# A smaller VectorE share of search work and a larger one of routing work per U tile; head-norm rows and positions in one transfer each

## The chip, the cores and the metric

One NeuronCore of a Trainium2 chip runs the kernel. TensorE (PE in the rows, PEld for its weight loads), VectorE (DVE), ScalarE (ACT), GpSimd (POOL) and SyncE (SP) each work through their own instructions in order, and wait for each other at semaphores; transfers are issued by SP alone and go through 16 DMA engines. The metric is the device time of one execution in microseconds (us); the lower the better. "Before" is the kernel without the change.

## The reference

One decoder layer on 256 tokens of width 1024: an input projection, two groups of attention heads, an output projection, and then a product-key expert layer (PEER). The change touches the gains of the head norms, the positions, and the search in PEER.

```python
proj = rmsnorm(x, norm1_gain) @ w_in            # split into two head groups
q = apply_rope(rmsnorm(q, q_gain), cos, sin)    # group A: 8 heads of 64; keys the same way
...
h = x + mixed
# PEER, 8 heads, 128 + 128 sub-keys each, 16384 experts
q = _rms((xt @ w_q).reshape(T, 8, 256))
s1, s2 = q_half1 . sub_keys1, q_half2 . sub_keys2
v1, i1 = top_k(s1, 16); v2, i2 = top_k(s2, 16)
vals, ci = top_k(v1[:, None] + v2[None, :], 16)
e = i1[ci // 16] * 128 + i2[ci % 16]; g = softmax(vals)
a = xt . expert_u[e]; y = (g * gelu(a)) @ expert_v[e]
```

## The kernel before

**No gather.** The expert part doesn't gather rows: it computes the scores of all 16384 experts for all 256 tokens (128 **U tiles** of 128 experts), multiplies them by a routing matrix that is zero except at the chosen experts, and multiplies the product with all of `peer_v` (128 V tiles). Products are made of float32 numbers split in two parts, `hi` (ACT, L769) and `lo` = value - hi (L772), so a U tile is 24 matmuls of 256 columns in three passes of eight: hi with hi, hi with lo, and last lo with hi (`xproj`, L1101). The `lo` of a tile is needed at its third pass, 16 matmuls after its start.

**The pipeline.** Step s of the loop issues the load of tile s+5, splits tile s+3 (`split`: hi on ACT, lo on POOL while `state["single"]` is true, else on DVE) and multiplies tile s; there are three buffers for loaded tiles and four for hi and for lo. 16 tiles of `peer_w_q` (queries) come first, then 128 U tiles (j = 0 to 127), then 128 V tiles (L1474).

**Work beside the tiles.** Between tiles, DVE does the rest of PEER, as a generator (`work_steps`) of pieces with a cost each, written down in the code: for each half of the tokens the search (`topk_steps`): 16 rounds over the sub-keys and 8 over the candidates (0.95 + 0.6 us each in the code's figures), both with `single` true; then, with `single` false, a few steps on indices (to L1253: "ranks"; L1256 to L1264: "cells"), the look-up of the indices (L1268 to L1277) and the softmax's end. Then three transposes on PE (`rT`), casts on DVE (L1297 to L1299), and the second half the same way. After both, 64 **routing groups** of 4 tokens: one-hot vectors on DVE (`oh`, L1305 and L1309), 8 matmuls on PE (`g`, L1317), and the product of the result with the columns of scores that are there already (`route_out`, L1330 on DVE; ACT copies it into columns that are still empty, L1332). From then on a pair of U tiles also has its scores multiplied by the routing columns on POOL (L1449). `work_for(share)` after each tile adds a share to a credit and takes pieces from the generator until the credit is used up:

```python
td = state["routed"]
work_for(2.95 - (1.3 if on_vector.get(s + 3) else 0))
```

So the share is 2.95 us a tile, less 1.3 if the tile's `lo` is on DVE. Where everything stands on each engine is set by this table of costs when the program is built. At U tile 4 a short block is put between (`sums`): the norms of the queries, with a power on POOL (`rq`, L151) between two DVE steps (L1378 to L1380 and L1383).

**The front of the kernel.** SP issues transfers in a written order. Three transfers (`load_gA`, L807 to L809) spread the gains of the head norms, one row of 64 numbers each, over 128 partitions and 8 + 2 + 2 heads (`gA`). They stand between the load of `wu` (L877) and that of the third weight group `win` (L258 called by `load_win(3)`), after which come `w2` and `load_win(4)`. `gB` (L856, 256 numbers of the same tensor to 128 partitions) is loaded earlier. DVE scales `gA` (L910) before it works on the gates and norms of the first projection (L381, L369, L372 to L377); ACT makes their sums (L366 to L368) and then the hi part of `win` (L279), and POOL its lo part (L274).

Of the kernel before, what the change touches and what calls it, by code (L numbers as in the profile page):

```python
# [48 lines left out]
P_N = 43  # L49


R_Q = 0
R_KS = 64
R_KW = 128
R_KC = 192
R_BQ = 256
R_BK = 352
R_N = 448

WIN_GROUPS = (256, 184, 256, 256, 256, 256, 256)  # L60

# [25 lines left out]
def body(tc, nc, ap, dbg=None):  # L87
    V, A, T, G, S = nc.vector, nc.scalar, nc.tensor, nc.gpsimd, nc.sync
# [6 lines left out]
    with ExitStack() as ctx:  # L95
# [33 lines left out]
        def accum(name):  # L129
            return acc.tile([128, 512], F32, tag="acc", name=name)  # L130
# [34 lines left out]
        x = xx[:, 0:2048].rearrange("p (t d) -> p t d", t=2)  # L165
# [4 lines left out]
        con = cst.tile([128, C_N], F32, name="con")  # L170
        ident = con[:, C_ID:C_ID + 128]
        one = con[:, C_ONE:C_ONE + 1]
        pp = cst.tile([128, P_N], F32, name="pp")
        posi = cst.tile([128, 3], I32, name="posi")
# [6 lines left out]
        w2 = wsm[:, 2560:2816].rearrange("p (a b n) -> p a b n", a=2, b=2)  # L181
        gA = wsm[:, 2816:3584].rearrange("p (h d) -> p h d", h=12)
# [557 lines left out]
        raws, parts, pend, on_vector = {}, {}, {}, {}  # L740
# [37 lines left out]
        h = x  # L778
        hs = nc.dram_tensor("hs", (256, 1024), F32, kind="Internal").ap()

        with tc.manual_schedule():

            def load_x(tt):
                for q in range(2):
                    S.dma_start(out=x[:, tt, q * 512:(q + 1) * 512], in_=ap["x"][tt * 128:(tt + 1) * 128, q * 512:(q + 1) * 512])

            win = {}

            def load_win(gi):
                win[gi] = load_pack(ap["win"][:, offs[gi]:offs[gi + 1]], WIN_GROUPS[gi], "win", 2 if gi else 4)  # L790

            def open_win(gi):
                win[gi] = split_pack(win[gi], 2 + gi % 2, WIN_GROUPS[gi], "win%d" % gi)

            def split_win(gi, q, e, what="hl"):
                win[gi][1](q, e, what)

            def load_pos():
                for tt in range(2):
                    S.dma_start(out=posi[:, tt:tt + 1], in_=bass.AP(tensor=ap["pos"].tensor, offset=tt * 128, ap=[[1, 128], [1, 1]]))  # L800
                for g in range(2):
                    S.dma_start(out=posi[g * 32:g * 32 + 15, 2:3], in_=bass.AP(tensor=ap["pos"].tensor, offset=31, ap=[[16, 15], [1, 1]]))

            rows = ap["rows"].tensor

            def load_gA():
                S.dma_start(out=gA[:, 0:8, :], in_=bass.AP(tensor=rows, offset=R_Q, ap=[[0, 128], [0, 8], [1, 64]]))  # L807
                S.dma_start(out=gA[:, 8:10, :], in_=bass.AP(tensor=rows, offset=R_KS, ap=[[0, 128], [0, 2], [1, 64]]))
                S.dma_start(out=gA[:, 10:12, :], in_=bass.AP(tensor=rows, offset=R_KW, ap=[[0, 128], [0, 2], [1, 64]]))  # L809

            def sumsq(tt, e):
                if e is A:
                    A.activation(out=r_sq2(), in_=x[:, tt, :], func=AF.Square, accum_out=ss1[:, tt:tt + 1])
                else:
                    V.scalar_tensor_tensor(r_sq2(), x[:, tt, :], 1.0, x[:, tt, :], op0=ALU.mult, op1=ALU.mult, accum_out=ss1[:, tt:tt + 1])

            def norm1():
                rsqrt(rs1, ss1, 1024.0, 128, 2)
                V.tensor_scalar(nrs1, rs1, -1.0, None, op0=ALU.mult)
                V.tensor_copy(rsrep, rs1[:, :, None].broadcast_to((128, 2, 128)))  # L820

            def masks():
                V.tensor_copy(trim, con[:, C_TRI:C_TRI + 128])
                V.tensor_copy(idb, ident)

            def w0(q, e, what):
                win[0][1].part(q, e, what)

            G.memset(posi, 0)
            G.memset(cm[:, 2048:3328], 0.0)  # L830
            A.activation(out=misc[:, 118:119], in_=mhalf[:, 0:1], func=AF.Square)
            tx = [transposed_split(x[:, tt, :], P_G1, xnT, tt, (lambda k, n, a=(fe, scrB)[tt]: a[:, k * 128:(k + n) * 128].rearrange("p (k t) -> p k t", k=n)), lo=V) for tt in range(2)]
            lows = [accum("low"), accum("low")]
            ss1 = small([128, 2], "n_ss")
            low0 = lambda tt: do(mm_pack(lows[tt][:, 0:256], tt, win[0][0]))
            load_x(0)
            S.dma_start(out=ident, in_=ap["con"][:, C_ID:C_ID + 128])
            S.dma_start(out=pp, in_=ap["pp"])
            load_x(1)
            load_win(0)  # L840
            open_win(0)
            next(tx[0])
            next(tx[0])
            next(tx[0])
            next(tx[0])
            w0(0, G, "h")
            w0(1, G, "h")
            load_win(1)
            open_win(1)
            next(tx[1])  # L850
            next(tx[1])
            w0(1, G, "l")
            do(tx[0])
            next(tx[1])
            w0(2, G, "h")
            S.dma_start(out=gB, in_=bass.AP(tensor=rows, offset=R_KC, ap=[[0, 128], [1, 256]]))  # L856
            next(tx[1])
            sumsq(1, V)
            w0(2, V, "l")
            load_pos()  # L860
            load_win(2)
            w0(3, G, "h")
            split_win(1, 0, None, "h")
            split_win(1, 1, None, "h")
            w0(3, V, "l")
            w0(0, G, "l")
            G.memset(Z, 0.0)
            G.memset(zer, 0.0)
            S.dma_start(out=con[:, 128:C_N], in_=ap["con"][:, 128:C_N])
            split_win(1, 1, G, "l")  # L870
            do(tx[1])
            sumsq(0, A)
            split_win(1, 0, V, "l")
            low0(0)
            V.tensor_scalar(gB[:, 64:160], gB[:, 64:160], float(np.float32(96 ** -0.5)), None, op0=ALU.mult)
            norm1()
            S.dma_start(out=wsm[:, 0:2560], in_=ap["wu"])  # L877
            masks()
            rope_tables()
# [472 lines left out]
        def work_for(share):  # L1352
            credit[0] = min(credit[0] + share, 4.0)
            while credit[0] > 0:
                c = next(work, None)
                if c is None:
                    break
                credit[0] -= c
# [61 lines left out]
        for s in range(NQ, NQ + NU):  # L1420
            j = s - NQ
            load(s + 5)
            split(s + 3)
            if s % 2 == 0:
                b = bank("a")
            xproj(b[:, (s % 2) * 256:(s % 2) * 256 + 256], s, xtT)
            if j == 126:
                for _ in work:
                    pass
                wsplit(0)  # L1430
                wsplit(1)
            if j == 0:
                pend["scores"]()
                qsum = sums()
            if j in (2, 4):
                next(qsum)
            if s % 2:
                td = state["routed"]
                dst = col(j - 1, 2)
                bv = b.rearrange("p (j t) -> p j t", j=2)  # L1440
                if td < 256:
                    A.activation(out=dst[:, :, td:], in_=bv[:, :, td:], func=AF.Gelu_apprx_tanh)  # L1442
                if td > 0:
                    if j < 127:
                        a = ring.tile([128, 2, 256], F32, tag="w", name="gl", bufs=2)
                    else:
                        a = raw("gl")[:, 0:512].rearrange("p (j t) -> p j t", j=2)
                    A.activation(out=a[:, :, :td], in_=bv[:, :, :td], func=AF.Gelu_apprx_tanh)  # L1448
                    (G if j < 127 else V).tensor_tensor(dst[:, :, :td], a[:, :, :td], dst[:, :, :td], op=ALU.mult)  # L1449
                state["done"] = j + 1  # L1450
            td = state["routed"]
            work_for(2.95 - (1.3 if on_vector.get(s + 3) else 0))


        ya = [[bank("y") for n in range(2)] for tt in range(2)]
# [36 lines left out]
def layout(x, positions, norm1_gain, w_in,  # L1492
# [5 lines left out]
    n = np.asarray  # L1498
# [8 lines left out]
    win = np.concatenate([w[:, :, g].transpose(1, 0, 2).reshape(128, -1) for g in groups], axis=1)  # L1507
# [2 lines left out]
    pp = np.concatenate([col(norm1_gain, 8), col(norm2_gain, 8), oga, col(out_gain_b, 4),  # L1510
                         col(mla_q_lora_gain, 2), col(mla_kv_lora_gain, 1),
                         n(cmp_pos)[0].reshape(16, 128).T], axis=1)
    rows = np.concatenate([n(v)[0] for v in (nsa_q_gain, nsa_ks_gain, nsa_kw_gain, nsa_kc_gain, mla_q_gain, mla_k_gain)])[None, :]
    wukv = n(mla_w_ukv)[0].reshape(128, 8, 2, 64).transpose(0, 2, 1, 3).reshape(128, 1024)
    wu = np.concatenate([n(mla_w_uq)[0].reshape(2, 128, 768).transpose(1, 0, 2).reshape(128, 1536), wukv], axis=1)
    w1 = np.stack([n(m)[0].reshape(16, 128, 256).transpose(1, 0, 2).reshape(128, 4096) for m in (cmp_k_w1, cmp_v_w1)])
# [6 lines left out]
    keys = n(peer_sub_keys)[0].reshape(16, 128, 128).transpose(2, 0, 1).reshape(128, 2048)  # L1523
    u = n(peer_u)[0].reshape(128, 128, 8, 128).transpose(1, 3, 2, 0).reshape(128, 128, 1024)
    v = n(peer_v)[0].reshape(128, 131072)
    d = dict(x=n(x)[0], pos=n(positions), con=_constants(), pp=pp, rows=rows, win=win, wu=wu, w1=w1, w2=w2,
             wout=wout, wq=wq, keys=keys, u=u, v=v)
    return {k: np.ascontiguousarray(a) for k, a in d.items()}

# [20 lines left out]
```

## Time and profile before

| | |
|---|---|
| time, median of 3 runs | 981.76 us (980.24 to 984.21) |
| the profiled execution | 981.5 us, of which the span of the profile is 979.7 us |
| PE busy | 944.3 us (96%) |
| DVE busy | 723.3 us (74%) |
| ACT, POOL busy | 500.4 us (51%), 185.4 us (19%) |
| DMA, mean rate over the span | 170 GB/s |

The span runs from the first to the last instruction of the profiled execution; some 1.8 us of its time lie outside. Busy shares are means over stages that differ: the front and attention (to 176 us), queries (to 219.5), U tiles (to 627.5) and V tiles.

### The profile page before, as it was taken

Reading aid. Unit: us, or ns where it says so; the run is one execution under the profiler, and the core shown is the slowest. Engines: PE = TensorE matmul, PEld = TensorE weight load, DVE = VectorE, ACT = ScalarE, POOL = GpSimd, SP = SyncE. Lnnn points to the kernel's source line nnn. Section 1 sums busy time; section 2 is a strip of 40 time slices with the busy share of each in tenths; the row PEclk is TensorE's granted clock in tenths of the full one; section 3 lists DMA queues with packets and bytes.
Section 4 is the critical chain, followed back from the end, with each engine's and each line's share of the span. In section 5 each row is a group of like instructions: output and inputs, shape, how many; then the busy total and the mean of one; then the engine's idle time right before and its main releaser. Section 6 shows DMA issues by size and latency. Waiting matters only on the chain.

```text
span 979.7 us, 17225 instructions
## 1 busy us (share of the span) xinstructions
PE 944.3 (96%) x6657; PEld 853.9 (87%) x6657; DVE 723.3 (74%) x1403; ACT 500.4 (51%) x924; POOL 185.4 (19%) x151
## 2 busy tenths in 40 slices
PE   7699899999899899999999999999999999999998
PEld 6587678999899899999999999988888888888886
DVE  6577988777989987888889997566666666666664
ACT  4445766656355445454544444455555555555552
POOL 5462524267049000000111111100000000000000
PEclk9899999999899899999999999999999999999999
DMA  7623421654466375455555555566665666566554
GB/s 239 211 89 103 175 66 52 207 169 134 151 207 198 115 214 170 154 157 166 159 169 166 155 155 181 180 193 194 193 194 193 194 194 193 194 193 194 193 195 149
DMA packets 48958, 166.74 MB, mean 170 GB/s; under 512 B 7276, under 2 KB 8300, under 8 KB 48620
## 3 DMA queue, kind: packets, MB, share of 16 engines
q1 hardware_dynamic: 48876, 165.64, 53.5%
q8 instruction: 52, 0.85, 0.3%
q14 instruction: 30, 0.25, 0.1%
HBM read 163.52 MB, written 2.10 MB: 169 GB/s over the span
## 4 chain that ended last, share of the span: by engine, by line
PE 77%; DVE 11%; DMA 5%; POOL 3%; ACT 1%; issue 1%; SPq 1%; DVEq 0%; POOLq 0%; ACTq 0%
PE y L1474 36%; PE a L1101 28%; PE q L1101 4%; PE g L1317 3%; DMA win<-win 3%; PE wo L980 1%; DVE lo L772 1%; DMA raw<-u 1%; PE s L1410 1%; PE ak L316 1%; POOL b_rs L151 1%; DMA B<-keys 1%; DVE B L1217 1%; DVE B L1218 1%; PE oA L697 1%
## 5 line engine op out<-in xcount | busy, mean ns | idle before, releaser
L772 DVE TENSOR_TENSOR lo<-raw,hi 128x1024 fp32r<-128x1024 f32 x238 | 291.2, 1227 | 96.2 <-ACT hi L769 94.3
L769 ACT ACTIVATE hi<-raw 128x1024 fp32r<-128x1024 f32 x266 | 280.0, 1054 | 56.8 <-DMA raw<-u 52.5
L1474 PE MATMUL y<-hi,w 128*128 128x512 f32 x1024 | 274.6, 389 | 0.0
L1101 PE MATMUL a<-xtT,hi 128*128 128x256 f32 x2048 | 268.2, 284 | 0.0
L1101 PEld LDWEIGHTS a<-xtT,hi 128*128 128x128 f32 x2048 | 250.6, 191 | 0.4 <-issue 0.4
L1474 PEld LDWEIGHTS y<-hi,w 128*128 128x128 f32 x1024 | 192.0, 188 | 40.1 <-ACT w L1204 0.2
L1474 PE MATMUL y<-lo,w 128*128 128x512 f32 x512 | 158.4, 389 | 0.0
L1101 PE MATMUL a<-xtT,lo 128*128 128x256 f32 x1024 | 142.4, 282 | 8.1 <-DVE lo L772 8.1
L1204 ACT ACTIVATE w<-B 128x256 fp32r<-128x256 f32 x128 | 53.5, 418 | 171.2 <-PE y L1474 171.1
L1101 PEld LDWEIGHTS a<-xtT,lo 128*128 128x128 f32 x1024 | 130.6, 192 | 8.5 <-DVE lo L772 8.5
L1474 PEld LDWEIGHTS y<-lo,w 128*128 128x128 f32 x512 | 96.1, 188 | 20.0
L1205 DVE TENSOR_TENSOR w<-B,w 128x256 fp32r<-128x256 f32 x128 | 54.4, 426 | 70.1 <-ACT w L1204 70.1
L1449 POOL TENSOR_TENSOR B<-gl,B 128x512 f32<-128x512 f32 (+37 forms) x40 | 32.0, 801 | 273.7 <-ACT gl L1448 273.7
L772 POOL TENSOR_TENSOR lo<-raw,hi 128x1024 fp32r<-128x1024 f32 x28 | 67.3, 2410 | 47.1 <-ACT hi L769 46.7
L1332 ACT ACTIVATE B<-g 128x64 f32<-128x64 f32 (+32 forms) x120 | 24.2, 250 | 72.6 <-DVE B L1330 72.6
L1442 ACT ACTIVATE B<-a 128x512 f32<-128x512 f32 (+37 forms) x60 | 27.7, 461 | 62.6 <-PE a L1101 62.6
L1305 DVE TENSOR_TENSOR oh<-misc,con 128x1024 f16<-128x1024 f16 x64 | 57.2, 894 | 0.0
L1309 DVE TENSOR_TENSOR oh<-oh,gf 128x1024 f16<-128x1024 f16 x64 | 45.2, 707 | 2.2
L1330 DVE TENSOR_TENSOR B<-g,B 128x448 f32<-128x448 f32 (+28 forms) x70 | 32.2, 466 | 18.2 <-ACT B L1442 18.1
L1317 PE MATMUL g<-oh 128*128 128x128 f16 x512 | 39.7, 220 | 0.0
L1101 PE MATMUL q<-xrT,hi 128*128 128x256 f32 x256 | 35.4, 284 | 0.0
L1101 PEld LDWEIGHTS q<-xrT,hi 128*128 128x128 f32 x256 | 32.0, 189 | 0.0
(317 smaller groups left out, 904.7 us busy)
## 6 DMA issues: line engine op xcount, KB each, us to landing
raw<-u SPq DMA_DIRECT2D x128, 512.0 KB, 3.6
raw<-v SPq DMA_DIRECT2D x128, 512.0 KB, 4.2
raw<-wq SPq DMA_DIRECT2D x16, 512.0 KB, 4.1
win<-win SPq DMA_DIRECT2D x10, 512.0 KB, 8.7
w<-w SPq DMA_DIRECT2D x8, 512.0 KB, 5.0
wo<-wout SPq DMA_DIRECT2D x8, 512.0 KB, 6.0
wsm<-wu SPq DMA_DIRECT2D x1, 1280.0 KB, 8.0
xx<-x SPq DMA_DIRECT2D x4, 256.0 KB, 3.3
```

What stands on the lines that cost most here:

```text
L769: A.activation(out=hi, in_=src, func=AF.Copy)
L772: e.tensor_tensor(lo, src, hi.bitcast(F32), op=ALU.subtract)
L1101: T.matmul(out, lhsT=w[:, k, :], rhs=xT[:, k, q, :], start=(n == 0 and k == 0), stop=(n == 2 and k == 7))
L1204: A.activation(out=w[:, 0, :], in_=b, func=AF.Copy)
L1205: V.tensor_tensor(w[:, 1, :], b, w[:, 0, :].bitcast(F32), op=ALU.subtract)
L1305: V.tensor_tensor(o[:, 0:2].rearrange("p a t (i two) -> p (a t) i two", two=2), iot.rearrange("p (i two) -> p i two", two=2)[:, None].broa ...
L1309: V.tensor_tensor(pairs(o[:, 2:4]), pairs(o[:, 1:2]).broadcast_to((128, 2, 4, 64, 2)), gf[:, t4, :, :, None, :].broadcast_to((128, 2, 4, 6 ...
L1317: T.matmul(b[:, i, :], lhsT=o[:, 0, i, :], rhs=o[:, 2 + q, i, :], start=(q == 0), stop=(q == 1))
L1330: V.tensor_tensor(w, bv[:, c0:m, :], w, op=ALU.mult)
L1442: A.activation(out=dst[:, :, td:], in_=bv[:, :, td:], func=AF.Gelu_apprx_tanh)
L1449: (G if j < 127 else V).tensor_tensor(dst[:, :, :td], a[:, :, :td], dst[:, :, :td], op=ALU.mult)
L1474: T.matmul(ya[tt][n], lhsT=wh[:, q, tt * 128:(tt + 1) * 128], rhs=src[:, n * 512:(n + 1) * 512], start=(jj == 0 and p == 0), stop=(jj == 1 ...
```

## The change

The share of a U tile becomes 2.65 us while nothing is routed yet, and 3.2 us once routing has begun (2.95 in both before). The row of gains is laid out on the host with each gain repeated as often as it has heads, so that `gA` comes in one transfer of 768 numbers to each partition; and the positions come as one array of 128 x 3, so that one transfer takes the place of four, and POOL no longer clears `posi` first.

```diff
             def load_pos():
-                for tt in range(2):
-                    S.dma_start(out=posi[:, tt:tt + 1], in_=bass.AP(tensor=ap["pos"].tensor, offset=tt * 128, ap=[[1, 128], [1, 1]]))
-                for g in range(2):
-                    S.dma_start(out=posi[g * 32:g * 32 + 15, 2:3], in_=bass.AP(tensor=ap["pos"].tensor, offset=31, ap=[[16, 15], [1, 1]]))
+                S.dma_start(out=posi, in_=ap["pos"])
...
             def load_gA():
-                S.dma_start(out=gA[:, 0:8, :], in_=bass.AP(tensor=rows, offset=R_Q, ap=[[0, 128], [0, 8], [1, 64]]))
-                S.dma_start(out=gA[:, 8:10, :], in_=bass.AP(tensor=rows, offset=R_KS, ap=[[0, 128], [0, 2], [1, 64]]))
-                S.dma_start(out=gA[:, 10:12, :], in_=bass.AP(tensor=rows, offset=R_KW, ap=[[0, 128], [0, 2], [1, 64]]))
+                S.dma_start(out=gA, in_=bass.AP(tensor=rows, offset=R_Q, ap=[[0, 128], [1, 768]]).rearrange("p (h d) -> p h d", h=12))
...
-            G.memset(posi, 0)
...
-            work_for(2.95 - (1.3 if on_vector.get(s + 3) else 0))
+            work_for((3.2 if td else 2.65) - (1.3 if on_vector.get(s + 3) else 0))
...
-    rows = np.concatenate([n(v)[0] for v in (nsa_q_gain, nsa_ks_gain, nsa_kw_gain, nsa_kc_gain, mla_q_gain, mla_k_gain)])[None, :]
+    rows = np.concatenate([n(nsa_q_gain)[0]] * 8 + [n(nsa_ks_gain)[0]] * 2 + [n(nsa_kw_gain)[0]] * 2
+                          + [n(v)[0] for v in (nsa_kc_gain, mla_q_gain, mla_k_gain)])[None, :]
```

In the built program the order of the front changes on SP alone (and by the missing clear on POOL). SP, from the second load of positions to that of `w2`, before (`win` are weight groups, `con` constants, `wsm` the buffer that holds `wu` and the gains):

```order
L802 DMA posi<-pos 15x1 x2
L258 DMA win<-win 128x1024 x2
L869 DMA con<-con 128x544
L877 DMA wsm<-wu 128x2560
L807 DMA wsm<-rows 128x8x64
L808 DMA wsm<-rows 128x2x64
L809 DMA wsm<-rows 128x2x64
L258 DMA win<-win 128x1024 x2
L917 DMA wsm<-w 128x256
```

and now:

```order
L257 DMA win<-win 128x1024 x2
L862 DMA con<-con 128x544
L870 DMA wsm<-wu 128x2560
L803 DMA wsm<-rows 128x768
L257 DMA win<-win 128x1024 x2
L910 DMA wsm<-w 128x256
```

The three transfers of gains have become one of 128 runs of 768 numbers; the order of the others is kept.

DVE, at the end of the second search (the 128x1024 rows are `lo` of U tiles; the CAST of 128x512 ends the ranks, the second CAST of 128x256 in the piece the cells), before:

```order
L1248 TENSOR_TENSOR B<-B,rq 128x128
L1252 TENSOR_SCALAR B<-B 128x128 x3
L1253 CAST B<-B 128x512
L1256 SCALAR_TENSOR_TENSOR B<-B 128x128
L1257 SCALAR_TENSOR_TENSOR B<-B 128x128
L1259 CAST B<-B 128x256
L1261 SCALAR_TENSOR_TENSOR B<-B 128x128 x3
L1262 SCALAR_TENSOR_TENSOR B<-B 128x128
L1263 SCALAR_TENSOR_TENSOR B<-B 128x128
L1264 CAST B<-B 128x256
L772 TENSOR_TENSOR lo<-raw,hi 128x1024 x2
```

and now:

```order
L1241 TENSOR_TENSOR B<-B,rq 128x128
L1245 TENSOR_SCALAR B<-B 128x128 x3
L1246 CAST B<-B 128x512
L771 TENSOR_TENSOR lo<-raw,hi 128x1024
L1249 SCALAR_TENSOR_TENSOR B<-B 128x128
L1250 SCALAR_TENSOR_TENSOR B<-B 128x128
L1252 CAST B<-B 128x256
L1254 SCALAR_TENSOR_TENSOR B<-B 128x128 x3
L1255 SCALAR_TENSOR_TENSOR B<-B 128x128
L1256 SCALAR_TENSOR_TENSOR B<-B 128x128
L1257 CAST B<-B 128x256
L771 TENSOR_TENSOR lo<-raw,hi 128x1024 x2
```

The first `lo` on DVE after the second search was that of tile 35, behind the cells; it is now that of tile 39, ahead of them, and the last one before the search is that of tile 23 instead of tile 20. At the end of the first search the rows of DVE are the same in both, but the first `lo` there is that of tile 10 instead of tile 9, and the block `sums` stands one round of the candidates' search earlier in DVE's row (it follows the fourth round instead of the fifth).

POOL, from the last query tiles to the first products with routing columns, before (`rq` is the power of `sums`):

```order
L1403 TENSOR_TENSOR B<-B 128x256
L772 TENSOR_TENSOR lo<-raw,hi 128x1024 x5
L151 TENSOR_TENSOR rq<-rs_x,mhalf 128x16
L772 TENSOR_TENSOR lo<-raw,hi 128x1024 x15
L1449 TENSOR_TENSOR B<-gl,B 128x2x8
```

and now:

```order
L1396 TENSOR_TENSOR B<-B 128x256
L771 TENSOR_TENSOR lo<-raw,hi 128x1024 x5
L150 TENSOR_TENSOR rq<-rs_x,mhalf 128x16
L771 TENSOR_TENSOR lo<-raw,hi 128x1024 x17
L1442 TENSOR_TENSOR B<-gl,B 128x2x4
```

Two more `lo` are POOL's: one in the first search, one in the second. On PE the first group of routing matmuls follows U tile 51 instead of 44, and the last one tile 116 instead of 118, so that 64 groups stand in 66 tiles instead of 75.

## Rows read from the trace of the kernel before

**Rows 1.** The page's first line, and the chain that ended last, by engine.

```profile
span 979.7 us, 17225 instructions
...
PE 77%; DVE 11%; DMA 5%; POOL 3%; ACT 1%; issue 1%; SPq 1%; DVEq 0%; POOLq 0%; ACTq 0%
```

**Rows 2.** Busy time by window: from:to, length, engines, clock, DMA share, GB/s.

```profile
60.00:176.00 116.00, 108.20 (x874) 89.70 (x872) 94.44 (x264) 72.75 (x217) 47.12 (x41) 1.00 0.32 109
247.00:259.00 12.00, 8.27 (x50) 8.07 (x48) 11.52 (x36) 2.60 (x3) 0.00 (x0) 0.72 0.40 124
...
580.00:602.00 22.00, 22.00 (x209) 21.53 (x209) 21.46 (x28) 9.49 (x18) 4.41 (x4) 1.00 0.51 164
```

**Rows 3.** PE in order of time at the two waits among the U tiles.

```profile
246.90 1.98 PE L1101 MATMUL a<-xtT,hi 128*128 128x256 f32 x16
252.60 2.07 PE L1101 MATMUL a<-xtT,lo 128*128 128x256 f32 x8 [3.73 <-DVE lo L772]
...
259.00 1.98 PE L1101 MATMUL a<-xtT,hi 128*128 128x256 f32 x16
...
324.65 1.98 PE L1101 MATMUL a<-xtT,hi 128*128 128x256 f32 x16
331.02 2.08 PE L1101 MATMUL a<-xtT,lo 128*128 128x256 f32 x8 [4.40 <-DVE lo L772]
...
337.47 1.98 PE L1101 MATMUL a<-xtT,hi 128*128 128x256 f32 x16
```

**Rows 4.** The chain in order of time, at the front: start, length, what.

```profile
18.23 20.25 DMA win<-win
```

**Rows 5.** DMA view of 0 to 60, then packets of 10.5 to 12.5, 20 to 37, 37 to 42.

```profile
wsm<-rows SPq DMA_DIRECT2D x1, 256.0 KB, 19.6
...
DMA packets 592, 0.47 MB, mean 234 GB/s; under 512 B 360, under 2 KB 488, under 8 KB 592
...
DMA packets 1724, 1.38 MB, mean 81 GB/s; under 512 B 1414, under 2 KB 1495, under 8 KB 1722
...
DMA packets 580, 1.99 MB, mean 398 GB/s; under 512 B 60, under 2 KB 107, under 8 KB 579
```

**Rows 6.** ACT and DVE at the front, in order of time: start, length, engine, line.

```profile
28.83 0.21 ACT L367 ACTIVATION_READ_ACCUMULATOR fe<-low,misc 128x1 f32 x1
...
30.57 0.25 ACT L368 ACTIVATION_READ_ACCUMULATOR fe<-low,misc 128x1 f32 x1
...
33.08 0.43 DVE L910 TENSOR_SCALAR wsm<-wsm 128x512 f32<-128x512 f32 x1 [6.62 <-DMA wsm<-rows]
...
33.99 0.17 DVE L150 TENSOR_SCALAR rs_x<-l_ss 128x2 f32<-128x2 f32 x1
```

**Rows 7.** POOL and DVE at `sums` in the first search.

```profile
239.94 2.92 POOL L151 TENSOR_TENSOR rq<-rs_x,mhalf 128x16 f32<-128x16 f32 x1 [1.40 <-DVE rs_x L150]
...
242.89 2.51 DVE L1383 TENSOR_SCALAR rq<-rq,misc 128x8 f32<-128x8 f32 x2 [3.03 <-POOL rq L151]
```

**Rows 8.** DVE around the second search: last `lo` before it, cells, first `lo` after.

```profile
279.21 1.23 DVE L772 TENSOR_TENSOR lo<-raw,hi 128x1024 fp32r<-128x1024 f32 x1 [1.37 <-ACT hi L769]
...
327.43 0.29 DVE L1256 SCALAR_TENSOR_TENSOR B<-B 128x128 f32<-128x128 f32 x1
...
329.75 2.35 DVE L772 TENSOR_TENSOR lo<-raw,hi 128x1024 fp32r<-128x1024 f32 x2
```

**Rows 9.** The chain's last nine U tiles, without routing groups.

```profile
602.19 25.50 PE a L1101 x216
```

**Rows 10.** POOL and DVE in two routing tiles.

```profile
566.52 1.12 POOL L1449 TENSOR_TENSOR B<-gl,B 128x424 f32<-128x424 f32 x1 [5.61 <-ACT gl L1448]
...
563.74 0.68 DVE L1305 TENSOR_TENSOR oh<-misc,con 128x1024 f16<-128x1024 f16 x1
...
566.80 1.38 DVE L1305 TENSOR_TENSOR oh<-misc,con 128x1024 f16<-128x1024 f16 x1
```

**Rows 11.** PE's longest wait between 60 and 176 us.

```profile
70.94 1.05 PE L461 MATMUL bT<-con,scrB 128*96 128x128 f32 x8 [1.83 <-DVE scrB L341]
```

More of the change, by code (lines that the diff above doesn't have):

```diff
@@ L52 @@
 R_Q = 0
[L53 to L58, printed above, removed]
+R_KC = 768
+R_BQ = 832
+R_BK = 928
+R_N = 1024
 WIN_GROUPS = (256, 184, 256, 256, 256, 256, 256)
@@ L1512, in layout @@
                          n(cmp_pos)[0].reshape(16, 128).T], axis=1)
-    rows = np.concatenate([n(v)[0] for v in (nsa_q_gain, nsa_ks_gain, nsa_kw_gain, nsa_kc_gain, mla_q_gain, mla_k_gain)])[None, :]
+    rows = np.concatenate([n(nsa_q_gain)[0]] * 8 + [n(nsa_ks_gain)[0]] * 2 + [n(nsa_kw_gain)[0]] * 2
+                          + [n(v)[0] for v in (nsa_kc_gain, mla_q_gain, mla_k_gain)])[None, :]
+    t = n(positions)[0]
+    ends = np.zeros(128, t.dtype)
+    for g in range(2):
+        ends[g * 32:g * 32 + 15] = t[31::16]
+    pos = np.stack([t[:128], t[128:], ends], axis=1)
     wukv = n(mla_w_ukv)[0].reshape(128, 8, 2, 64).transpose(0, 2, 1, 3).reshape(128, 1024)
@@ L1525, in layout @@
     v = n(peer_v)[0].reshape(128, 131072)
-    d = dict(x=n(x)[0], pos=n(positions), con=_constants(), pp=pp, rows=rows, win=win, wu=wu, w1=w1, w2=w2,
+    d = dict(x=n(x)[0], pos=pos, con=_constants(), pp=pp, rows=rows, win=win, wu=wu, w1=w1, w2=w2,
              wout=wout, wq=wq, keys=keys, u=u, v=v)
```

## The prediction

> **What bounds the kernel now.** I read the chain by engine first: 77% of the span is PE, 11% DVE and 5% transfers [rows 1]. PE's own work doesn't change here, so only time in which PE waits or runs slowly can be won. From 60 us on the view of waits leaves PE few of them, and among the U tiles just two, each for a `lo` of DVE: 3.73 us before the third pass of tile 9 and 4.40 us before that of tile 35 [rows 3]. The reader should see what else they cost. From 259.00 (start of tile 11) to 324.65 (start of tile 35) PE does 24 tiles and one set of transposes in 65.65 us: 2.72 us a tile and 0.37 for the transposes. But tiles 9 and 10 together take 259.00 - 246.90 = 12.10 us where two plain tiles take 5.44, and tiles 35 and 36 take 337.47 - 324.65 = 12.82. So the first place loses 6.66 us and the second 7.38, more than the waits: the window around the first shows a mean granted clock of 0.72 of 2.4 GHz [rows 2], so PE went on at the lower level (1.2 GHz) for a while after it had stood. Together they lose 14.0 us.
>
> The second thing is the front. The chain there has one piece of 20.25 us, the load of weight group 3, issued at 18.23 and there at 38.48 [rows 4]. It isn't the bytes: from 20 to 37 us the queue moved 1.38 MB at 81 GB/s, and 1414 of 1724 packets were under 512 B; right after, the same queue ran at 398 GB/s [rows 5]. The small ones are the gains: `gA` is 128 x 12 = 1536 runs of 256 B. Its first transfer took 19.6 us to land, and the weight group stands behind it. DVE waited 6.62 us for it at L910 [rows 6].
>
> **The front: -6.5 us.** One transfer of 128 runs of 3072 B takes the place of 1536 runs. The nearest row is `gB`, 128 runs of 1024 B from the same tensor, spread in the same way: all of them (488 - 360 = 128 packets from 512 B to 2 KB) lie in the 2 us from 10.5 to 12.5, in a full queue [rows 5]. By count the new one takes 2 us, by bytes three times that, 6 us. Either way it is there by 26 us, about when DVE gets to L910 (33.08 - 6.62 = 26.46), and the weight group's 1 MB follows in 2.6 us at 398 GB/s, at 29 at the latest.
>
> What is late next: DVE needs ACT's sums of the gates, which don't depend on the load; those of the first half are there at 28.83 + 0.21 = 29.04, so `rs_x` can start at 29.1 instead of 33.99 [rows 6]: 4.9 us. The cast of the weight group on ACT waits for the end of the sums (30.57 + 0.25 = 30.82) instead of the load (38.48): 7.7 us. Both lead into the same POOL and PE work, so the stage after it starts 4.9 to 7.7 us earlier; I take 6.5, between them. From there to the query tiles the chain is engine work in fixed order, and the DMA share is 0.32 [rows 2], so the shift should come through whole. The positions (four transfers to one, no clear on POOL) lie beside a full queue and cost or win nothing; without that cover it would be a few tenths.
>
> **The first search: -4.6 us.** With 2.65 instead of 2.95 a tile the generator is one tile behind, so the first `lo` on DVE, at the same place in DVE's row, is that of tile 10. It is due one tile later: tile 10 would start at 246.90 + 2.72 = 249.62, its third pass 1.81 later (16 of 24 matmuls), at 251.43. When does DVE get there? Before, PE's wait ended with it, at 252.60. `sums` now comes one round (1.55 us, the code's figure) earlier. POOL's power had started 1.40 after POOL was free, on a late DVE [rows 7]; it can now start about 1.3 earlier, and DVE leaves the block that much earlier, but has one more round behind it: 252.60 - 1.3 + 1.55 = 252.85, so PE waits 1.4 us instead of 3.73. Then DVE does the cells (329.75 - 327.43 = 2.32 [rows 8]) and a `lo` (1.12 from start to next start: two of 1.23 in 2.35 [rows 8]) and has tile 11 ready at 256.3; it is due after the eight matmuls left of tile 10 (0.91) and 1.81 more, at 255.57: 0.7 late. So 2.1 us of the 6.66 stay. Do short waits slow the clock? PE waited 1.83 us at 69 us [rows 11], and the clock of that stage stayed at 1.00 [rows 2]; so I count none. Were it to fall again, 2.9 (6.66 - 3.73) would stay too.
>
> **The second search: -7.2 us.** Before: the last `lo` ahead of it (tile 20) is done at 280.44, the first behind it (tile 35) at 329.75 + 1.23 = 330.98 [rows 8]: 50.5 us, while PE moves on by 15 tiles, 40.8. Tile 20's was due at 259.00 + 9 x 2.72 + 0.37 + 1.81 = 285.66, a lead of 5.2; 9.7 - 5.2 gives 4.5, and 4.40 was measured, so the account holds. Now 16 tiles lie between (23 to 39), 43.5 us, and the cells come after that `lo`, so DVE needs 50.5 - 2.3 = 48.2. It loses 4.7 of a lead of 5.2: no wait. The `lo` of tile 40 comes 2.32 + 1.12 = 3.44 behind, against 2.72: 0.2 late. POOL takes the additional `lo` at the pace of those before. So of 7.38 some 0.2 stay.
>
> **The routing: -0.5 us.** 64 groups now stand in 66 tiles. A tile with a group costs PE the same as before; the number of groups is the same. But a U tile without one takes 25.50 / 9 = 2.83 us after the routing [rows 9], and 2.72 before its start (above); why, no row tells. Seven more tiles fall before the start: -0.8 (0 if the pace belongs to something else). Against it, DVE has less room: at the end of the routing it is busy 21.46 of 22.00 us and PE still doesn't wait measurably [rows 2]. POOL's product with the routing columns lengthens one `oh` of two from 0.68 to 1.38 [rows 10]. Before, one tile in six or seven gave DVE a rest; now almost none. I add 0.3, with 0 and 3 (some 10 late pairs of tiles at 0.3) as bounds.
>
> **Sum.** 981.5 (the profiled execution's own time) - 6.5 - 4.6 - 7.2 - 0.5 = 962.7. The median is 0.3 above that execution, so I say 963. Bounds of the terms: front 0 to 7.7, first search 1.7 to 6.7, second 3 to 7.4.
>
> **The rivals.**
>
> *The gains stay slow.* If it is the bytes read again and again from one place, not the number of runs, that held the queue, 384 KB at the rate of before land when they did, and the front wins nothing: 969. For it: `gA` is the one load that is so slow, and all partitions read the same row; against it: `gB`, which does so too, wasn't. 12%. The Trainium skill has a rule near this one ("DMA: Bandwidth & Descriptors", Why small descriptors are slow): a run of 256 B loses some 27% to a fixed cost, which by itself would, as an estimate, bring the end of the gains from 37 to about 32 us and the kernel to some 968. The trace disagrees with it as the whole cause: 81 against 398 GB/s is a factor of five.
>
> *The wait moves on.* DVE is still late at the first search and PE falls to 1.2 GHz again (+2.9), or the lead before the second search is 2 to 3 us shorter than I take it, with a wait and its slow tiles again (+3 to 6): 966 to 969. For it: my margin there is 0.5 us. 17%.
>
> *Routing becomes DVE's.* If both `oh` of a pair of tiles ran beside POOL's product, a pair would cost DVE 0.7 more than PE gives it, and 32 pairs 22 us: 962.7 + 22 = 985, slower. It decides from 0.6 us a pair (19 / 32). Against it: the product comes once in two tiles and lasts 1.12 us [rows 10], in 6.7. 3%.
>
> *Nothing moves.* The front's shift is eaten by another load and the searches end as before: 978 to 986. No row speaks for it. 3%.
>
> **How the numbers follow.** The forecast, 958 to 967, has 65%. With the first two rivals, both at 966 to 970, it makes 94%, of which some fall out at either end; 957 to 970 should hold 8 in 10. All of these are faster by over 0.5% (4.9 us, about what a measurement of this kernel can tell from no change). Faster 0.94, same 0.03, slower 0.03.
>
> **What would show it.** Right: the gains land before 27 us and L910 waits for nothing; the load of weight group 3 falls out of the chain; the query tiles start some 6 us earlier; one or two waits of 0.5 to 1.5 us at tiles 10 and 11 and none over 1 us near tile 39; the granted clock at 1.00 through the U tiles; routing tiles as long as before. Wrong: a low clock near tile 10 or 39; packets under 512 B still between 20 and 37 us; PE waiting for `oh` in the routing.

## The result and the profile after

The changed kernel takes 969.04 us, the median of 6 runs (966.86 to 973.06); the kernel before, on the same chip, 981.32 (980.24 to 985.37). The ratio is 0.9874 (95%: 0.9855 to 0.9893): 12.4 us or 1.3% faster. The forecast was 963 with a range of 957 to 970: the right sign and inside the range, but only two thirds of the gain, and outside the 958 to 967 that the prediction gave to its own mechanism (65%): the time lies among those of the first two rivals. The profiled execution of the changed kernel is the fastest of its six (966.86, span 965.1), so the profiles differ by 14.6 where the medians differ by 12.3.

From here on lines are those of the changed kernel: L771 is the `lo` that was L772, L1376 the scaling of `rq` that was L1383, L903 the scaling of `gA` that was L910.

The page's first line and its chain by engine, after; they answer to [rows 1]:

```profile
span 965.1 us, 17209 instructions
...
PE 88%; DVE 8%; ACT 1%; POOL 1%; issue 1%; DMA 0%; SPq 0%; DVEq 0%; POOLq 0%; ACTq 0%
```

Transfers have gone from the chain. The DMA view of 0 to 60 us has the gains, and that of 20 to 37 the packets [rows 5]; then two rows of DVE in order of time (start, length, line), for [rows 6]:

```profile
wsm<-rows SPq DMA_DIRECT2D x1, 384.0 KB, 9.4
...
DMA packets 1134, 3.74 MB, mean 220 GB/s; under 512 B 128, under 2 KB 256, under 8 KB 1132
...
26.14 0.42 DVE L903 TENSOR_SCALAR wsm<-wsm 128x512 f32<-128x512 f32 x1
...
29.03 0.17 DVE L149 TENSOR_SCALAR rs_x<-l_ss 128x2 f32<-128x2 f32 x1
```

So far the front does what was forecast: the gains land 9.4 us after their issue, L903 waits for nothing, and `rs_x` starts at 29.03 where 33.99 was, 4.96 earlier. Then the gain shrinks. DVE and POOL, in order of time, a few us on:

```profile
32.73 1.24 DVE L371 TENSOR_SCALAR l_rr<-l_rr,misc 128x2 f32<-128x2 f32 x1 [0.64 <-POOL l_rr L150]
33.88 0.18 DVE L337 TENSOR_TENSOR fe<-krg,cm 128x32 f32<-128x32 f32 x1
33.98 1.23 DVE L338 TENSOR_TENSOR fe<-krg,cm 128x16 f32<-128x16 f32 x1
...
35.62 0.88 DVE L340 TENSOR_TENSOR misc<-fe 128x32 f32<-128x32 f32 x1
...
32.66 5.01 POOL L273 TENSOR_TENSOR win<-win,win 128x512 fp32r<-128x512 f32 x4
```

Operations that take about 0.2 us for the first half of the tokens (0.23, 0.17 and 0.18 in the same trace) take 1.24, 1.23 and 0.88 for the second, beside POOL's split of weight group 3, which the earlier load has brought to this place: 2.8 us. The projection `bk` behind them starts at 37.44, where it started at 39.62, so 2.2 earlier; PE before, then now:

```profile
39.62 1.20 PE L427 MATMUL bk<-wsm,scrB 128*128 128x512 f32 x2
...
37.44 2.04 PE L426 MATMUL bk<-wsm,scrB 128*128 128x512 f32 x2 [0.16 <-issue]
```

The clock was at half of 2.4 GHz for 10.2 us; busy time by window (from:to, length, engines, clock, DMA share, GB/s):

```profile
32.40:42.60 10.20, 6.53 (x13) 3.10 (x12) 9.78 (x16) 4.43 (x7) 9.20 (x11) 0.50 0.46 135
```

The kernel before had two such stretches, 33.0 to 39.6 and 46.8 to 50.1 us. The second stood behind a wait of PE of 2.10 and slowed the matmuls of `aq`; it did not come now. The rows of `aq`, then of the start of U tile 0 (215.47 instead of 219.56), before and now each time:

```profile
46.03 4.93 PE L316 MATMUL aq<-win,xnT 128*128 128x256 f32 x24
...
44.00 3.43 PE L315 MATMUL aq<-win,xnT 128*128 128x256 f32 x24
...
219.56 2.05 PE L1101 MATMUL a<-xtT,hi 128*128 128x256 f32 x16
...
215.47 2.05 PE L1094 MATMUL a<-xtT,hi 128*128 128x256 f32 x16
```

The searches, by PE's rows; the first `lo` behind the first search is that of tile 10 [rows 3], and one row of the chain has all of tiles 20 to 48:

```profile
245.53 1.98 PE L1094 MATMUL a<-xtT,hi 128*128 128x256 f32 x16
251.37 2.07 PE L1094 MATMUL a<-xtT,lo 128*128 128x256 f32 x8 [3.87 <-DVE lo L771]
253.25 2.48 PE L1094 MATMUL a<-xtT,hi 128*128 128x256 f32 x16
...
256.47 1.98 PE L1094 MATMUL a<-xtT,hi 128*128 128x256 f32 x16
...
278.72 78.93 PE a L1094 x696
```

The first search still costs a wait of 3.87, longer than before: tiles 10 and 11 take 256.47 - 245.53 = 10.94 where two plain ones take 5.44, a loss of 5.5 (6.66 before). The second is gone: 696 matmuls, 29 tiles, in 78.93 us, 2.72 each, through the place where 7.38 were lost. From tile 37 to the first V tile it was 290.06 before (627.53 - 337.47 [rows 3]) and is 288.27 (613.11 - 324.84); the V tile of before, then tile 37 and the V tile of now:

```profile
627.53 0.63 PE L1474 MATMUL y<-hi,w 128*128 128x512 f32 x2
...
324.84 1.98 PE L1094 MATMUL a<-xtT,hi 128*128 128x256 f32 x16
...
613.11 0.63 PE L1467 MATMUL y<-hi,w 128*128 128x512 f32 x2
```

| part, profile against profile | forecast | measured |
|---|---|---|
| front, to U tile 0 | -6.5 | -4.1 |
| first search | -4.6 | -1.2 |
| second search | -7.2 | -7.4 |
| routing, and the tiles behind it | -0.5 | -1.8 |

With 0.2 less at the end that is 14.6. These parts are of one pair of executions, and each can be off by a microsecond or two: `e1_shares` below, with the front of the kernel before, has its U tile 0 at 217.93, 1.6 earlier than that kernel, and seven profiles with the changed front have it between 214.76 and 217.57. What held the first search is in DVE's and POOL's rows [rows 7]:

```profile
234.97 2.92 POOL L150 TENSOR_TENSOR rq<-rs_x,mhalf 128x16 f32<-128x16 f32 x1 [0.51 <-DVE rs_x L149]
237.86 4.75 POOL L771 TENSOR_TENSOR lo<-raw,hi 128x1024 fp32r<-128x1024 f32 x2
...
237.92 4.72 DVE L1376 TENSOR_SCALAR rq<-rq,misc 128x8 f32<-128x8 f32 x2 [3.03 <-POOL rq L150]
```

Two operations on 128 x 8 numbers take 4.72 us, as long as the two `lo` of POOL that start with them; before, they took 2.51, beside one `lo` of 2.40. The second `lo` is the additional one that the first search now leaves to POOL.

### The profile page after: what moved, and what is told of

It reads as the page before. It is cut to its first block, busy times and chain, and to the rows that moved or that the text cites. A ratio compares the mean times of both kernels' runs of the same rounds, so it can differ in the third digit from the quotient of the medians.

```text
span 965.1 us, 17209 instructions
## 1 busy us (share of the span) xinstructions
PE 938.3 (97%) x6657; PEld 846.4 (88%) x6657; DVE 724.3 (75%) x1400; ACT 498.9 (52%) x921; POOL 187.0 (19%) x149
## 4 chain that ended last, share of the span: by engine, by line
PE 88%; DVE 8%; ACT 1%; POOL 1%; issue 1%; DMA 0%; SPq 0%; DVEq 0%; POOLq 0%; ACTq 0%
PE y L1467 36%; PE a L1094 35%; PE q L1094 5%; PE g L1310 3%; PE wo L973 1%; PE aq L315 1%; PE s L1403 1%; PE ak L315 1%; PE bq L434 1%; PE tx L297 1%; PE oA L696 0%; POOL lo L771 0%; DVE rq L1376 0%; PE sA L662 0%; PE pTA L685 0%
## 5 line engine op out<-in xcount | busy, mean ns | idle before, releaser
L771 DVE TENSOR_TENSOR lo<-raw,hi 128x1024 fp32r<-128x1024 f32 x236 | 289.4, 1228 | 96.3 <-ACT hi L768 94.1
L1094 PE MATMUL a<-xtT,hi 128*128 128x256 f32 x2048 | 264.1, 282 | 0.0
L1094 PEld LDWEIGHTS a<-xtT,hi 128*128 128x128 f32 x2048 | 246.6, 189 | 0.4 <-issue 0.4
L1094 PE MATMUL a<-xtT,lo 128*128 128x256 f32 x1024 | 140.2, 280 | 3.9 <-DVE lo L771 3.9
L1094 PEld LDWEIGHTS a<-xtT,lo 128*128 128x128 f32 x1024 | 128.5, 190 | 4.1 <-DVE lo L771 4.1
L771 POOL TENSOR_TENSOR lo<-raw,hi 128x1024 fp32r<-128x1024 f32 x30 | 72.2, 2419 | 52.1 <-ACT hi L768 51.8
L1442 POOL TENSOR_TENSOR B<-gl,B 128x512 f32<-128x512 f32 (+33 forms) x37 | 29.8, 806 | 256.8 <-ACT gl L1441 256.8
L1325 ACT ACTIVATE B<-g 128x64 f32<-128x64 f32 (+29 forms) x121 | 23.6, 244 | 76.8 <-DVE B L1323 76.8
L1435 ACT ACTIVATE B<-a 128x512 f32<-128x512 f32 (+33 forms) x59 | 28.1, 476 | 63.8 <-PE a L1094 63.7
L1323 DVE TENSOR_TENSOR B<-g,B 128x8 f32<-128x8 f32 (+32 forms) x69 | 32.8, 481 | 10.0 <-ACT B L1435 9.8
```

The costliest lines, as they stand in the source:

```text
L771: e.tensor_tensor(lo, src, hi.bitcast(F32), op=ALU.subtract)
L1094: T.matmul(out, lhsT=w[:, k, :], rhs=xT[:, k, q, :], start=(n == 0 and k == 0), stop=(n == 2 and k == 7))
L1323: V.tensor_tensor(w, bv[:, c0:m, :], w, op=ALU.mult)
```

## The experiments

The theory: a DVE operation that reads and writes SBUF stands still while POOL's `lo` runs, and starts when that ends; so L1376's two operations each waited out one `lo`, and the small operations of the front a piece of POOL's split each. The rival: the smaller share as such, or the shifted front, makes the wait at tile 10. All times are medians. A ratio compares all the runs of a kernel with runs of the kernel before on the same chip, and is not the quotient of two medians; the first four runs, e5 to e8, and e10 with e11 stand on three chips, so between these groups only ratios compare. Each kernel from the third on starts from one named in its expectation.

**e1_shares and e2_loads: the change in its two parts.** The first is the kernel before with the one line of the shares, the second the changed kernel with that line taken back.

```diff
-            work_for(2.95 - (1.3 if on_vector.get(s + 3) else 0))
+            work_for((3.2 if td else 2.65) - (1.3 if on_vector.get(s + 3) else 0))
```

> The shares alone (2.65 and 3.2), on the loads of before. By the terms as the two profiles showed them (front -4.1, first search -1.2, second search -7.4, routing and after it -1.8) the change loses only the front: 4.1 above the changed kernel, 973, U tile 0 at 219.5 as before, and L1376 again held over 4 us beside two POOL lo. The rival is that L1376 fell beside two lo because the front was shifted: then it takes about 2.5 as before, the first search gives its 4.6 and the time is 970.

> The loads alone (gains and positions in one transfer each), with 2.95 everywhere. If the front is worth what it showed, 4.1, and nothing later takes it back, 977, with the waits of about 3.7 and 4.4 still before a lo of VectorE in the two searches. The rival is that an earlier front is soaked up by those waits: 981. If the front could give the 6.5 that I counted, 975.

Measured: e1_shares 973.19 us, ratio 0.9923 (0.9896 to 0.9949); e2_loads 976.66, 0.9947 (0.9930 to 0.9964). By the ratios the parts are worth 7.6 and 5.2 us and add up to the whole (12.8 for 12.4) within their intervals of 2.6 and 1.7 us to either side; by the medians beside them (982.57 before) they are 9.4 and 5.9. In `e1_shares` U tile 0 was expected at 219.5 and started at 217.93. L1376 (here first e1_shares, on the old loads, where it is L1383, then e2_loads), in order of time:

```profile
240.06 4.72 DVE L1383 TENSOR_SCALAR rq<-rq,misc 128x8 f32<-128x8 f32 x2 [3.03 <-POOL rq L151]
```

```profile
239.48 2.50 DVE L1376 TENSOR_SCALAR rq<-rq,misc 128x8 f32<-128x8 f32 x2 [3.03 <-POOL rq L150]
```

The second `lo` beside it comes with the shares, not with the earlier front: the front as its cause falls.

**e3_rq_one and e4_rq_pool: the scaling of `rq` in another form, and on another engine.** `E` is V in the first and G (POOL) in the second.

```diff
-            for tt in range(2):
-                V.tensor_scalar(rq[:, tt * 8:tt * 8 + 8], rq[:, tt * 8:tt * 8 + 8], rs2[:, tt:tt + 1], None, op0=ALU.mult)
+            rqv = rq.rearrange("p (t m) -> p t m", t=2)
+            E.tensor_tensor(rqv, rqv, rs2[:, :, None].broadcast_to((128, 2, 8)), op=ALU.mult)
```

> The changed kernel with the scaling of rq (L1376) as one TENSOR_TENSOR of VectorE in place of two TENSOR_SCALARs. Theory: each of the two operations had to wait for one POOL lo (2.40 and 2.44), so one operation waits once: DVE leaves the sums about 2.4 earlier, the wait of 3.87 at tile 10 falls to about 1.5 and the time by 2.5 to 4, to 965 to 966.5. If a TENSOR_TENSOR is not held at all, 4.5 earlier: no wait over 0.5, 964. The rival, that the wait of 3.87 comes from the smaller search share and not from L1376: no change, 969.

> The changed kernel with the scaling of rq on POOL, behind its pow, so that DVE neither waits for the pow (3.03) nor is held beside the lo (4.72). Theory: DVE is 7 us earlier at the end of the first search, no wait of PE over 0.5 at tiles 10 and 11, no fall of the clock there: 5 us less, 964. POOL's next two lo come about 0.6 later, which PE does not see. The rival, that the smaller search share holds the wait: no change, 969.

Measured: 965.25 (0.9835; 0.9809 to 0.9862) and 964.84 (0.9829; 0.9804 to 0.9854). In e3_rq_one the one operation is held by one `lo`, and the wait is 1.49; DVE's row, then PE's at tile 10:

```profile
238.16 2.37 DVE L1376 TENSOR_TENSOR rq<-rq,misc 128x16 f32<-128x16 f32 x1 [3.03 <-POOL rq L150]
...
249.27 1.20 PE L1094 MATMUL a<-xtT,lo 128*128 128x256 f32 x8 [1.49 <-DVE lo L771]
```

In e4_rq_pool PE doesn't wait at all: a row of its chain runs from tile 5 to tile 20 without a piece of another engine.

```profile
231.25 42.41 PE a L1094 x360
```

So L1376 was the cause, to the size: 2.35 us off DVE's row took 2.4 off the wait, and with a single hold left the two waits are those of the forecast (1.49 and 0.44 for 1.4 and 0.7). The rival that the smaller share as such holds the wait has fallen.

**e8_all_295: the old share, with `rq` on POOL.** In e4_rq_pool:

```diff
-            work_for((3.2 if td else 2.65) - (1.3 if on_vector.get(s + 3) else 0))
+            work_for(2.95 - (1.3 if on_vector.get(s + 3) else 0))
```

> The kernel of e4_rq_pool with 2.95 throughout, as before the change. Theory: the first search's wait is that of rq and goes without the smaller share too (no wait over 0.5 near tile 10), while the second search's wait, which only the smaller share removes, stays at 3.8 to 4.4 with its slow clock, about 7: 972. If the smaller share is needed for the first search as well, a wait of 1 to 2 there and 974 to 976.

Measured: 971.94 (0.9906; 0.9884 to 0.9929), no wait at tiles 9 to 11, and at the second search:

```profile
321.91 2.08 PE L1094 MATMUL a<-xtT,lo 128*128 128x256 f32 x8 [5.10 <-DVE lo L771]
```

The two stalls have two causes: with `rq` on POOL the first goes without the share, the second only with it. The share's part of the gain is the second search.

**e7_route_295: 2.65 and 2.95.** In e4_rq_pool:

```diff
-            work_for((3.2 if td else 2.65) - (1.3 if on_vector.get(s + 3) else 0))
+            work_for((2.95 if td else 2.65) - (1.3 if on_vector.get(s + 3) else 0))
```

> The kernel of e4_rq_pool with 2.65 in the search and 2.95 (not 3.2) in the routing. Theory: a routing tile is set by PE's own extra matmuls, not by the share, and 64 of them stand before tile 126 either way, so the time is the same within 1.5 us, 964 to 966. The rival, that the larger routing share gave part of the 1.8 that I had not counted: 966.5.

Measured: 965.05 (0.9824; 0.9800 to 0.9848), the same as e4_rq_pool. So the routing share is worth nothing that shows beside intervals of 2.4 us to either side. But its profile has a wait of 1.24 at tile 39, where e4_rq_pool, whose program is the same to that place, has none. DVE's sums of candidates (L1222), in e4_rq_pool and in e7_route_295:

```profile
307.78 1.08 DVE L1222 TENSOR_TENSOR B<-B 128x256 f32<-128x256 f32 x3
```

```profile
309.55 5.51 DVE L1222 TENSOR_TENSOR B<-B 128x256 f32<-128x256 f32 x3
```

In e4_rq_pool POOL was between two `lo` at that moment; in e7_route_295 a `lo` started at 309.68 and two of the three sums waited one out each. In e4_rq_pool the `lo` of tile 39 was done 3.5 us before PE's third pass (323.82 for 327.33); the 4.43 us more on DVE used that lead up. So one program can have executions with and without the wait, by where POOL stands; that this makes the spread of the six runs (6 us) was not tried.

**e6_gain_three: is it the run or the number of transfers?**

```diff
-                S.dma_start(out=gA, in_=bass.AP(tensor=rows, offset=R_Q, ap=[[0, 128], [1, 768]]).rearrange("p (h d) -> p h d", h=12))
+                for a, b in ((0, 8), (8, 10), (10, 12)):
+                    S.dma_start(out=gA[:, a:b, :], in_=bass.AP(tensor=rows, offset=R_Q + a * 64, ap=[[0, 128], [1, (b - a) * 64]]).rearrange("p (h d) -> p h d", h=b - a))
```

> The kernel of e4_rq_pool, with the gains in three transfers again, but out of the widened row, so of runs of 2048, 512 and 512 bytes. If the length of a run set the 19.6 us of before, they still land within 10 us of their issue, L903 does not wait, and the time is 965 as in e4_rq_pool. If the number of transfers set it, they land 5 us later, L903 waits again and the time is 968 to 970.

Measured: 963.92 (0.9825; 0.9805 to 0.9844). The first of three lands after 9.6 us where the same 256 KB took 19.6 [rows 5]:

```profile
wsm<-rows SPq DMA_DIRECT2D x1, 256.0 KB, 9.6
```

The layout of the row was the cause; that three transfers became one is worth nothing. What about the layout is open: with runs of 256 B the same 256 B are also read 1024 times, with runs of 2048 B only 128 times, and no run here has short runs from different places. For the repeated reading speaks, without showing it, that 360 packets under 512 B passed in 2 us beside a mean of 234 GB/s earlier in the same queue, where the stretch of the gains had 1414 in 17 us at 81 GB/s [rows 5].

**e5_rot_pool, e10_blocks_dve, e11_win6_dve: taking the holds out of the front.** First the rotation of the small key part goes to POOL (the helper `rotate` takes the engine as `e`):

```diff
-            rotate(krg[:, None, :], 1, 16, tt, 1, dst=rkr[:, tt, None, :])
+            rotate(krg[:, None, :], 1, 16, tt, 1, dst=rkr[:, tt, None, :], e=G)
```

> The kernel of e4_rq_pool, with the rotation of low_post (L337 to L340, which only b_proj's L446 needs) on POOL, ahead of its split of the fourth weight group (L273). Theory: DVE's small operations at 33 to 37 us stand on the path of bk and are held by that split (L371 1.23, L338 1.23, L340 0.86 in place of about 0.2 each); without them DVE reaches L376 about 2.9 earlier, bk starts at about 34.9 instead of 37.8 and the queries' tiles 2 to 3 earlier: 962. The rival, that the split of the fourth group or a later transfer holds the front in their place: under 0.7, 964 to 965.

Measured: 961.25 (0.9797; 0.9776 to 0.9818). `bk` starts at 34.79 (37.76 in e4_rq_pool), and the clock of 32 to 60 us is 1.00 where e4_rq_pool had 0.88. But in the profile U tile 0 starts at 214.10 for 214.76, so 2.3 of the 3 us are given back, in one wait on DVE's rotation of the queries, which hangs on POOL's row, and behind which the clock fell to half from 65.6 to 68.7 us. The two profiles are 0.9 apart where the medians are 3.6 (3.1 by the ratios, which is about their noise), for that of e4_rq_pool is of its fastest run. PE, then POOL:

```profile
65.51 1.91 PE L460 MATMUL bT<-con,scrB 128*96 128x128 f32 x8 [5.03 <-DVE scrB L340]
...
33.93 5.99 POOL L273 TENSOR_TENSOR win<-win,win 128x512 fp32r<-128x512 f32 x4
39.88 4.27 POOL L407 TENSOR_TENSOR cm<-cm,pp 128x120 f32<-128x120 f32 x8
44.12 2.90 POOL L150 TENSOR_TENSOR b_rs<-rs_x,mhalf 128x16 f32<-128x16 f32 x1
```

The power that DVE waits for (`b_rs`) stands behind L407. So the next two take work off POOL:

```diff
-                        G.tensor_tensor(blk[:, v, ch * 8:ch * 8 + 8, g, 0:15],
+                        V.tensor_tensor(blk[:, v, ch * 8:ch * 8 + 8, g, 0:15],
...
-            split_win(6, 1, G)
+            split_win(6, 1, V)
```

> The kernel of e5_rot_pool with the eight additions of blocks (L407, 4.27 of POOL at 39.9) on DVE, which stood idle for 4.5 before L445 waiting for POOL's power. Theory: after e5_rot_pool POOL's row bounds the front; the power starts at once when its input is there (about 42.4 instead of 44.1), what follows it comes about 1.7 earlier, PE's wait of 5.03 before the third bT falls to 3 to 3.5, and the time to 959.5. The rival, that the additions on DVE, held by POOL's split, only move the delay: 961.

> As e10_blocks_dve, and the second half of the last weight group's split (L273 at 61.3) on DVE too, so that L477 (1.22) and L338 (1.35) at 61 to 64 are held by nothing. Theory: 2 us more before the third bT, so the wait there falls to 1 to 1.5 and the time to 957.5. The rival: DVE's extra lo of 1.2 and the changed order behind it take it back, 959.5.

Measured: e10_blocks_dve (the first line alone) 959.71 (0.9795; 0.9773 to 0.9816), e11_win6_dve (both) 956.95 (0.9762; 0.9745 to 0.9779). The times are as expected, but by the ratios the first is only 0.2 better than e5_rot_pool, which is nothing beside the noise; e11_win6_dve is clear of it. The way of the first is not the one expected: its power started at 42.90 and took 3.82, so L445 came only 0.3 earlier. The wait at `bT` still fell from 5.03 to 0.58, for two other reasons: what it waits for came 2.1 earlier, since L477 and L338 took 0.23 and 0.28 and were through when POOL's last split started at 61.61, and PE itself came 2.3 later (its second `bT` started at 61.55 for 59.21), with the clock at half from 34 to 38 us. In e11_win6_dve the same wait is 1.58 (1 to 1.5 expected); PE's row, and the chain of its page:

```profile
61.76 0.51 PE L460 MATMUL bT<-con,scrB 128*96 128x128 f32 x3 [1.58 <-DVE scrB L340]
...
PE 91%; DVE 6%; ACT 1%; POOL 1%; issue 1%; DMA 0%; SPq 0%; DVEq 0%; POOLq 0%; ACTq 0%
```

Its clock is 1.00 over the whole span. It beats the kernel before by 2.4% and the changed one by about 1.1%: taking DVE's small steps and POOL's work out of each other's way was worth about as much as the change itself.

## Why the prediction was right, and where not

**The front: mechanism right, size off (-6.5 for -4.1).** The step that failed is "so the stage after it starts 4.9 to 7.7 us earlier". The layout of the row was the cause (e6_gain_three), the gains land and `rs_x` moves by 4.96 as worked out. But an earlier weight group also brings POOL's split of it earlier, beside DVE's second half, where 2.8 us of holds leave a shift of 37.44 - 39.62 = -2.2 at `bk`. Behind it the shift did not only come through whole, it grew: to 3.5 at the second `bk` (47.27 for 50.80), as the second stretch at half clock did not come (1.5 us of `aq`), and to 4.1 at U tile 0. That the holds stood on the path to `bk`, e5_rot_pool showed (34.79 for 37.76). By the ratio the loads alone gave 5.2 (e2_loads), with an interval of 3.5 to 6.9: the times by themselves do not rule out 6.5, but the stage did not start 4.9 us or more earlier.

**The first search: a step failed (-4.6 for -1.2).** The account had `sums` start earlier, and so "DVE leaves the block that much earlier", 1.3 us. The power did come earlier against POOL (a wait of 0.51 instead of 1.40, so 0.9; L1373's two operations ahead of it, held too, took 1.14 where they had taken 0.48), but the block behind it became 2.21 longer (4.72 for 2.51): DVE left 1.3 us later, not earlier. That puts the wait at 1.4 + 2.6 = 4.0; it was 3.87. The gain of 1.2 is below even the bound of 1.7 that the term had. The row was in view: L1383 at 2.51 for two operations of 128 x 8 [rows 7] is a price that calls for a reason, and the additional `lo` of POOL was read from the order, but not set beside it. The rival "the wait moves on" had the outcome, 966 to 969, at 17%, and the fall of the clock with it: the granted clock fell to half (1.2 GHz) at the end of PE's wait of 3.87 us, as the window there (columns as above) shows.

```profile
250.80:254.30 3.50, 2.93 (x13) 2.93 (x14) 3.36 (x11) 0.00 (x0) 0.00 (x0) 0.51 0.50 150
```

In e3_rq_one, with a wait of 1.49, it stayed at 1.00, as I had taken it for short waits. Two microseconds already go either way: behind a wait of 2.02 at 70.15 us e4_rq_pool has a mean of 0.66 from 70 to 75, behind one of 2.03 at 68.16 us e10_blocks_dve stays at 1.00. The window of e3_rq_one from 240 to 262:

```profile
240.00:262.00 22.00, 20.07 (x174) 19.68 (x173) 21.07 (x61) 9.22 (x11) 2.86 (x2) 1.00 0.52 168
```

The Trainium skill has the rule that I left out ("SBUF — State Buffer", Who interferes with whom): a DVE instruction with two SBUF inputs, or a copy or `tensor_scalar` in its two-port mode, shares a port pair with POOL, and whoever comes second is blocked for the other's whole instruction. The traces agree: 2.37 for one `tensor_tensor` of 128 x 16 behind one `lo`, 4.72 for two operations behind two. From the rows, as an estimate, the second `lo` costs 2.2 us, and the slower clock behind a wait so long some 1.6 (the loss of 5.5 less the wait of 3.87): with both, 962.7 would have become 966.5.

**The second search: right (-7.2 for -7.4),** with room to spare, part of it luck: the lead that I put at 0.5 us (5.2 less 4.7) was 3.5, as the `lo` of tile 39 was done at 327.40 + 1.22 = 328.62 and PE's third pass needed it at 332.09. From the last `lo` before the search (done at 282.28) to this one DVE took 46.3 us and not 48.2, because the sums of candidates were hardly held this time (1.09 us for 3.29 before; the cast ahead of them was held 0.45 more). The rest is a longer lead ahead of the search. The sums before, then now, and the two rows of tile 39:

```profile
310.27 3.29 DVE L1229 TENSOR_TENSOR B<-B 128x256 f32<-128x256 f32 x3
...
312.54 1.09 DVE L1222 TENSOR_TENSOR B<-B 128x256 f32<-128x256 f32 x3
...
327.40 1.22 DVE L771 TENSOR_TENSOR lo<-raw,hi 128x1024 fp32r<-128x1024 f32 x1
...
332.09 1.07 PE L1094 MATMUL a<-xtT,lo 128*128 128x256 f32 x8
```

Held by one `lo` more, 2.2 longer, it would still have been enough; held by two, as in e7_route_295, it was not.

**The routing: -0.5 for -1.8, not by the share.** Of it 0.8 was the pace of seven more tiles at 2.72. The rest is the pace of the tiles behind the routing, 2.73 where [rows 9] had 2.83; e4_rq_pool has 2.72 there too and e5_rot_pool and e6_gain_three 2.83 in the same order of PE, so it isn't the change's (e1_shares, with the same shares, has 2.83 too). The rival that routing becomes DVE's did not come: routing tiles take 3.34 as before.

**The gains stay slow:** this rival fell; the gains are there 9.4 us after their issue.

## What to carry to other kernels

When a transfer or a share moves work earlier, ask which engine that work runs on and what it will then stand beside: here POOL's `lo` stopped DVE's smallest operations for its whole length, and an operation of 0.2 us that shows 2.5 in a profile is the sign. Keep a tiny step behind another engine's result on that engine, so that the critical one need neither wait for it nor be held. A row that is spread over the partitions should lie whole in memory: 256 KB landed 19.6 us after their issue in runs of 256 B, and 9.6 in runs of 2048 B, behind the same load in the queue.

## What was not expected of the hardware

DVE's searches are not held: MAX8, FIND_INDEX8 and MATCH_REPLACE8 take 0.24 to 0.26 us in the first search's rounds over the candidates beside a `lo` of POOL as without one, while in the same stretch L1376 is held 2.4 us each time. So POOL beside DVE is free or very dear by the kind of DVE's operation, which the busy time of neither engine tells.

A U tile takes 2.72 us in some stretches and 2.83 in others, at a granted clock of 1.00: in e4_rq_pool 2.83 for the 15 tiles to 20 (42.41 us, where e5_rot_pool has 40.82) and 2.72 after; the next row of its chain has 29 tiles.

```profile
273.98 78.91 PE a L1094 x696
```

In these traces the pace changes where tiles have waits or other matmuls between them, and is then kept. What sets it stays open; two profiles can differ by 1 to 2 us by it alone.
